# NaN-ignoring row maximum: seven loads, each cut into 27 quarter rows and one quarter row that is itself cut by partitions

## The chip, the cores and the metric

The kernel runs on one core of a Trainium2 chip. A core has engines that each run their own list of instructions and signal each other by semaphores. Four matter here: ScalarE (ACT in the profile), GpSimd (POOL), VectorE (DVE) and SyncE (SP), which here only issues transfers. Sixteen DMA engines move the data between the chip's main memory and the on-chip memory of 128 partitions. The metric is the device time of one execution in microseconds (us). The kernel before has a median of 1252.84 us over three runs (1252.82 to 1252.95).

## The reference

```python
batch, seq, dim = 32, 2048, 2048
x = np.random.randn(batch, seq, dim).astype(np.float32)
mask = np.random.rand(batch, seq, dim) < 0.1
x[mask] = np.nan
...
return np.nanmax(x, axis=axis).astype(np.float32)
```

The axis is the last one. So 65,536 rows of 2,048 floats (537 MB) are read, and one maximum per row is written, NaNs left out.

## The kernel before, in words

**Tiling.** `TILES` is a list of 74 tiles. The unit is a quarter row, `Q` = 512 floats (2,048 bytes). A common tile has 28 quarters, 7 rows, for each of the 128 partitions: 57,344 bytes per partition. A tile is written as three lists, `(loads, pieces, reds)`, whose sums are equal: how the transfer is cut, how the cleaning of NaNs is cut, and how the reductions are cut. The common one is `([28], [7, 9, 12], [16, 12])`: one load, three pieces, two reductions. `GROUPS` joins tiles that share one block of rows; in it each partition owns consecutive rows.

**Stages of a tile.** (1) SyncE issues the tile's loads into one of three buffers `xt` (`BUFS`, line 307). (2) For each piece ScalarE turns the upper 16 bits of each float into a key `kt` (lines 375 and 226), a mapping in which NaN saturates. (3) GpSimd turns the key back into upper bits and writes them into the tile (lines 396 and 236), so that NaNs have become a very low number. A piece with a minus sign in `TILES`, such as the -7 in `[9, 12, -7]`, is turned back by ScalarE itself (`release`, line 350). (4) VectorE reduces the cleaned rows by maximum into `acc` (line 421, noted as line 243). At the end of the rows of some groups `find` marks rows that held only NaNs, and at the very end SyncE stores `acc`.

**What sets the order.** Every engine runs its list in the order of the program text; `Order.add` puts the semaphore waits on. A load waits for two things, `before + lanes[turn]` (line 310): `before` is the last reduction of the tile that used this buffer, three tiles ago; `lanes[turn]` is the transfer that used the same one of 14 landing semaphores (`LANES`), 14 issues ago. A piece on ScalarE waits for the loads that overlap it (`here`, line 365) and for a free key buffer (three of 12 quarters each). A reduction waits for the pieces that it covers.

**Stages of the run.** Tile 0 has one row. Tiles 1 to 47 are common ones, but every eighth (8, 16, 24, 32, 40) is `([28], [9, 12, -7], [8, 20])`, in which ScalarE relieves GpSimd of 7 quarters. Tiles 48 to 61 vary the pieces a little. From tile 62 on the loads are cut smaller and smaller, down to one of 1 quarter (256 KB) in tile 72, and more pieces go back through ScalarE.

The change touches the tiles with the numbers 26, 28, 30, 32, 34, 56 and 58. Before, 26, 28, 30 and 34 are common ones; 32 is `([28], [9, 12, -7], [8, 20])`; 56 is `([28], [7, 9, 12], [12, 16])`; 58 is `([28], [6, 10, 12], [16, 12])`.

Of the kernel before, what the change touches and what calls it, by code (L numbers as in the profile page):

```python
# [8 lines left out]
D = 2048  # L9

Q = D // 4
# [4 lines left out]
TILES = (  # L16
    [([4], [4], [4])]
    + [([28], [7, 9, 12], [16, 12])] * 7
    + [([28], [9, 12, -7], [8, 20])]
    + [([28], [7, 9, 12], [16, 12])] * 7  # L20
    + [([28], [9, 12, -7], [8, 20])]
    + [([28], [7, 9, 12], [16, 12])] * 7
    + [([28], [9, 12, -7], [8, 20])]
    + [([28], [7, 9, 12], [16, 12])] * 7
# [23 lines left out]
)  # L48

GROUPS = [TILES[i : i + 15] for i in range(0, 60, 15)] + [TILES[60:73], TILES[73:]]  # L50


# [12 lines left out]
LANES = 14  # L65
# [7 lines left out]
EDGE = TOP + 0.25  # L73

NONE = -255.0 * 2.0**120


def total(pieces):
    return sum(sum(map(abs, p)) if isinstance(p, tuple) else abs(p) for p in pieces)
# [93 lines left out]
def kernel(  # L173
# [15 lines left out]
    nc = tc.nc  # L189
    P = nc.NUM_PARTITIONS  # L190
# [9 lines left out]
    xr = x.bitcast(i32).flatten_outer_dims()  # L200
    R = xr.shape[0]
    of = out.bitcast(i32).flatten_outer_dims().rearrange("r c -> (r c)")
    rows = [sum(sum(loads) for loads, _, _ in g) * Q // D for g in GROUPS]
    assert R == P * sum(rows)

    sing = ctx.enter_context(tc.tile_pool(name="sing", bufs=1))
# [12 lines left out]
    with tc.tile_critical():  # L219
        order = Order(nc)  # L220
# [61 lines left out]
        number = 0  # L282
        lanes = [[] for _ in range(LANES)]
        turn = 0
# [4 lines left out]
        for gi, (s, g) in enumerate(zip(rows, GROUPS)):  # L289
# [4 lines left out]
            acc = accs[:, first : first + s]  # L294
            base = 0
            for loads, pieces, reds in g:
                assert sum(loads) == total(pieces) == sum(reds)
                xt, before = xts[number % BUFS], free[number % BUFS]
                number += 1
                landed = []  # L300
                at = 0
                for c in loads:
                    c *= Q
                    e = order.add(
                        "sp",
                        nc.sync,
                        lambda: nc.sync.dma_start(  # L307
                            out=xt[:, at : at + c], in_=xg[:, base + at : base + at + c]
                        ),
                        before + lanes[turn],  # L310
                        lane=f"load{turn}",
                        step=16,
                    )
                    lanes[turn] = [e]
                    turn = (turn + 1) % LANES
                    landed.append((at, at + c, e))
                    at += c
                clean = []
                after = []
                at = done = 0  # L320
                reds = [n * Q for n in reds]
                part = []
                held = []
                pairs = {}
                if number not in APART:
                    pairs = joints(pieces, [n // Q for n in reds])
                flat = sum((p if isinstance(p, tuple) else (p,) for p in pieces), ())
                half = {}
                piece = 0

                def cleaned(a, b, k, i, e):

                    nonlocal clock
                    clock += 1
                    both = [(a, b, k, flat[i] < 0, clock)]
                    if i in pairs:
                        if pairs[i] not in half:
                            half[pairs[i]] = both
                            return
                        both += half.pop(pairs[i])  # L340
                    for a, b, k, back, when in both:
                        kfree[k].append((back, when, e))
                        clean.append((a, b, e))

                def name(i):
                    return f"pair{number}_{pairs[i][0]}" if i in pairs else None

                def release():
                    for a, b, k, kp, e, i in held:
                        e = act(  # L350
                            [e],
                            name(i),
                            out=xt[:, a:b].bitcast(i16)[:, 1::2],
                            in_=kp,
                            func=ACT.Copy,
                            bias=float(TOP),
                            scale=-1.0,
                        )
                        cleaned(a, b, k, i, e)
                    held.clear()  # L360

                for parts in pieces:
                    parts = parts if isinstance(parts, tuple) else (parts,)
                    c = int(sum(map(abs, parts))) * Q
                    here = [l for a, b, l in landed if a < at + c and b > at]
                    kold = []
                    if used + c > KEYS:
                        key = (key + 1) % NKEYS
                        used = 0
                        kold, kfree[key] = last(kfree[key]), []  # L370
                        assert all(k != key for q in half.values() for _, _, k, _, _ in q)
                        if at + c == sum(loads) * Q:

                            kold = kold + last(kfree[(key + 1) % NKEYS])
                    e_key = act(
                        here + kold,
                        out=kts[key][:, used : used + c],
                        in_=xt[:, at : at + c].bitcast(i16)[:, 1::2],
                        func=ACT.Prelu,
                        bias=top,  # L380
                        scale=-1.0,
                        alpha=float(TOP - LOW) / (EDGE - NAN),
                    )
                    release()
                    for c in parts:
                        back, wait, c = c < 0, isinstance(c, float), int(abs(c)) * Q
                        kp = kts[key][:, used : used + c]
                        used += c
                        to = xt[:, at : at + c].bitcast(i16)[:, 1::2]
                        at += c  # L390
                        if back:
                            held.append((at - c, at, key, kp, e_key, piece))
                            if not wait or at == sum(loads) * Q:
                                release()
                        else:
                            e = pool(
                                [e_key],
                                name(piece),
                                out=to,
                                in0=kp,  # L400
                                scalar1=-1.0,
                                scalar2=float(TOP),
                                op0=ALU.mult,
                                op1=ALU.add,
                            )
                            cleaned(at - c, at, key, piece, e)
                        piece += 1
                        open_ = [h[0] for h in held] + [p[0] for q in half.values() for p in q]
                        while reds and done + reds[0] <= min([at] + open_):
                            n = reds.pop(0)  # L410


                            lo = done - 1 if done % D else done
                            done += n
                            row = (base + lo) // D
                            if done % D:
                                m, to = 1, xt[:, done - 1 : done].bitcast(f32)
                            else:
                                m = max(n // D, 1)
                                to = acc[:, row : row + m]  # L420
                            e = dve(
                                [e for a, b, e in clean if b > lo and a < done] + part,
                                nc.vector.tensor_reduce,
                                out=to,
                                in_=xt[:, lo:done]
                                .bitcast(f32)
                                .rearrange("p (c d) -> p c d", c=m),
                                axis=mybir.AxisListType.X,
                                op=ALU.max,
                            )  # L430
                            part = [e] if done % D else []
                            after.append(e)
                free[(number - 1) % BUFS] = after[-1:]
                base += at
# [17 lines left out]
        for (og, bits), e in zip(stores, ready):  # L452
# [5 lines left out]
                lane="store",  # L458
# [40 lines left out]
```

## Time and profile before

| | |
|---|---|
| median of three runs | 1252.84 us |
| profiled execution, span from first to last instruction | 1251.3 us |
| VectorE, ScalarE, GpSimd busy | 1110.8, 986.6, 1168.6 us |
| mean duration of a 7, 9 and 12 quarter piece on ScalarE | 3.28, 4.12, 5.41 us |
| the same on GpSimd | 4.20, 5.34, 7.04 us |
| reduction of 16 and of 12 quarters on VectorE | 8.69, 6.54 us |
| read from main memory | 536.87 MB, 429 GB/s over the span |
| loads, and the median from issue to landing of a 28-quarter load | 105; 22.5 us |

The profile comes from one execution with the hardware profiler on; its span has no launch or finish in it, so it is a little shorter than the measured time. Engine names in its lines are ACT, POOL, DVE and SP; SPq is SyncE's queue of transfers. "L236" is the line of the helper that issued the instruction. A line such as `L243 DVE TENSOR_REDUCE acc<-xt` is an operation that reads `xt` and writes `acc`. A load is carried as packets: the trace's records have 128 of them for each load, one per partition, each as long as the partition's part of it. A load has landed when its semaphore has been raised sixteen times, once by each DMA engine; the trace has each of these times.

### The profile page before, as it was taken

To read this page: it belongs to the slowest core of one execution; us is meant where nothing else is said; L and a number is where in the kernel's file an instruction comes from. 1 tells how busy PE (TensorE), PEld (TensorE's weight loads), DVE (VectorE), ACT (ScalarE), POOL (GpSimd) and SP (SyncE) were. 2 spreads that over 40 slices of the span, in tenths; PEclk is the share of its full clock that TensorE was granted. 3 is DMA by queue.
4 is the path that set the end of the run, shared out by engine and by line. 5 is a ranking of instruction groups with operands and counts; after the bars stand their busy time and mean duration, and the time that the engine had idled before them with its cause. 6 is when DMAs were issued, how large, how long until landed. Compare 5 with 4: busy or idle time off the path is not lost.

```text
span 1251.3 us, 893 instructions
## 1 busy us (share of the span) xinstructions
DVE 1110.8 (89%) x181; ACT 986.6 (79%) x273; POOL 1168.6 (93%) x242
## 2 busy tenths in 40 slices
DVE  0888989888889888898988888998888899999999
ACT  3777887778787877788777878777777878999998
POOL 2999989998999899998999899999999999989998
DMA  9999999999999999999999999999999999999997
GB/s 415 440 412 438 440 440 440 411 440 440 440 436 415 440 440 436 438 416 440 440 436 438 416 440 440 436 438 416 440 440 435 440 416 436 436 431 430 428 428 295
DMA packets 15991, 537.20 MB, mean 429 GB/s; under 512 B 2544, under 2 KB 2544, under 8 KB 3568
## 3 DMA queue, kind: packets, MB, share of 16 engines
q1 hardware_dynamic: 15984, 537.14, 99.3%
q14 instruction: 7, 0.06, 0.0%
HBM read 536.87 MB, written 0.26 MB: 429 GB/s over the span
## 4 chain that ended last, share of the span: by engine, by line
DMA 36%; DVE 30%; POOL 20%; ACT 13%; issue 1%; SPq 0%; ACTq 0%
DMA xt<-in_x_dram 36%; DVE acc L243 30%; POOL xt L236 20%; ACT kt L226 11%; ACT xt L226 2%; SPq L307 0%; DVE none L249 0%; DVE acc L263 0%; SPq L494 0%; ACTq L158 0%; SPq L219 0%
## 5 line engine op out<-in xcount | busy, mean ns | idle before, releaser
L236 POOL TENSOR_SCALAR xt<-kt 128x3584 int16<-128x3584 uint16 (+11 forms) x236 | 1167.5, 4947 | 77.9 <-ACT kt L226 60.1
L243 DVE TENSOR_REDUCE acc<-xt 128x3 f32<-128x6144 f32 (+4 forms) x175 | 1107.6, 6379 | 136.7 <-POOL xt L236 128.8
L226 ACT ACTIVATE kt<-xt,scalars 128x3584 uint16<-128x3584 int16 (+9 forms) x247 | 935.3, 3825 | 257.7 <-DMA xt<-in_x_dram 241.6
L226 ACT ACTIVATE xt<-kt 128x512 int16<-128x512 uint16 (+6 forms) x24 | 52.8, 2202 | 0.7
L226 ACT ACT_TABLE_LOAD x1 | 1.3, 1283 | 0.9 <-SPq L219 0.9
L243 DVE TENSOR_REDUCE xt<-xt 128x1 f32<-128x1536 f32 x1 | 1.7, 1745 | 0.0
L269 DVE MEMSET scalars<- 128x1 f32 x1 | 0.1, 59 | 1.0 <-SPq L219 1.0
L249 DVE TENSOR_SCALAR none<-acc 128x414 int32<-128x414 f32 (+1 forms) x2 | 0.8, 380 | 0.1
L263 DVE TENSOR_TENSOR acc<-acc,none 128x414 int32<-128x414 int32 (+1 forms) x2 | 0.7, 374 | 0.1
L249 POOL TENSOR_SCALAR late<-acc 128x91 int32<-128x91 f32 x1 | 0.5, 545 | 0.1
L263 POOL TENSOR_TENSOR acc<-acc,late 128x91 int32<-128x91 int32 x1 | 0.3, 340 | 0.1
L480 POOL MEMSET const-float32-0.0<- 128x1 f32 x1 | 0.1, 98 | 0.2 <-issue 0.2
L226 ACT ACTIVATE scalars<-scalars 128x1 f32<-128x1 f32 x1 | 0.2, 203 | 0.0
L480 POOL MEMSET const-bfloat16-1.0<- 128x1 bf16 x1 | 0.1, 101 | 0.0
L480 POOL MEMSET const-uint8-127<- 128x1 uint8 x1 | 0.1, 101 | 0.0
L480 POOL MEMSET const-float32-1.0<- 128x1 f32 x1 | 0.1, 99 | 0.0
## 6 DMA issues: line engine op xcount, KB each, us to landing
xt<-in_x_dram SPq DMA_DIRECT2D x61, 7168.0 KB, 22.5
xt<-in_x_dram SPq DMA_DIRECT2D x2, 5120.0 KB, 17.3
xt<-in_x_dram SPq DMA_DIRECT2D x3, 2816.0 KB, 22.5
xt<-in_x_dram SPq DMA_DIRECT2D x4, 2048.0 KB, 22.2
xt<-in_x_dram SPq DMA_DIRECT2D x5, 1536.0 KB, 29.0
xt<-in_x_dram SPq DMA_DIRECT2D x2, 3584.0 KB, 24.6
xt<-in_x_dram SPq DMA_DIRECT2D x6, 1024.0 KB, 26.6
xt<-in_x_dram SPq DMA_DIRECT2D x3, 1792.0 KB, 29.9
```

The source lines that it names most:

```text
L226: lambda: nc.scalar.activation(**kw),
L236: lambda: nc.gpsimd.tensor_scalar(**kw),
L243: return order.add("dve", nc.vector, lambda: do(**kw), deps)
L249: lambda: engine.tensor_scalar(out=none, in0=acc, scalar1=NONE, scalar2=float(0x00800000), op0=ALU.is_equal, op1=ALU.mult,),
L263: lambda: engine.tensor_tensor(out=bits, in0=bits, in1=none, op=op),
L269: e_top = order.add("dve", nc.vector, lambda: nc.vector.memset(top, EDGE), [])
L480: nc = _bacc.Bacc("TRN2", target_bir_lowering=False, num_devices=1)
```

## The change

Seven tiles get a common new form: loads of 27 quarters and of 1 quarter, pieces of 7, 9 and 12, reductions of 16 and 12. A load may now be a pair `(quarters, runs)`; the runs are numbers of partitions that add up to 128, and each run becomes a transfer of its own. So the last quarter row of the seven tiles comes in two transfers, the first for partitions 0 to 119, 125, 116, 107 or 87, the second for the rest. All other lines of the diff follow from the new form of `loads`: a helper `width` adds the quarters up.

```diff
+def parted(*runs):
+    return [([27, (1, runs)], [7, 9, 12], [16, 12])]
+
+
+for number, runs in (
+    (26, (120, 8)),
+    (28, (126, 2)),
+    (30, (117, 11)),
+    (32, (108, 20)),
+    (34, (88, 40)),
+    (56, (120, 8)),
+    (58, (126, 2)),
+):
+    TILES = TILES[:number] + parted(*runs) + TILES[number + 1 :]
...
+def width(loads):
+    return sum(c[0] if isinstance(c, tuple) else c for c in loads)
...
                 for c in loads:
+                    c, runs = c if isinstance(c, tuple) else (c, (P,))
+                    assert sum(runs) == P
                     c *= Q
-                    e = order.add(
-                        "sp",
-                        nc.sync,
-                        lambda: nc.sync.dma_start(
-                            out=xt[:, at : at + c], in_=xg[:, base + at : base + at + c]
-                        ),
-                        before + lanes[turn],
-                        lane=f"load{turn}",
-                        step=16,
-                    )
-                    lanes[turn] = [e]
-                    turn = (turn + 1) % LANES
-                    landed.append((at, at + c, e))
+                    p = 0
+                    for n in runs:
+                        e = order.add(
+                            "sp",
+                            nc.sync,
+                            lambda: nc.sync.dma_start(
+                                out=xt[p : p + n, at : at + c],
+                                in_=xg[p : p + n, base + at : base + at + c],
+                            ),
+                            before + lanes[turn],
+                            lane=f"load{turn}",
+                            step=16,
+                        )
+                        lanes[turn] = [e]
+                        turn = (turn + 1) % LANES
+                        landed.append((at, at + c, e))
+                        p += n
                     at += c
```

In the order of instructions, SyncE has 14 more transfers, ScalarE one operation fewer (the -7 of tile 32) and GpSimd one more; VectorE has as many as before.

More of the change, by code (lines that the diff above doesn't have):

```diff
@@ L202 @@
     of = out.bitcast(i32).flatten_outer_dims().rearrange("r c -> (r c)")
-    rows = [sum(sum(loads) for loads, _, _ in g) * Q // D for g in GROUPS]
+    rows = [sum(width(loads) for loads, _, _ in g) * Q // D for g in GROUPS]
     assert R == P * sum(rows)
@@ L296 @@
             for loads, pieces, reds in g:
-                assert sum(loads) == total(pieces) == sum(reds)
+                assert width(loads) == total(pieces) == sum(reds)
                 xt, before = xts[number % BUFS], free[number % BUFS]
@@ L371 @@
                         assert all(k != key for q in half.values() for _, _, k, _, _ in q)
-                        if at + c == sum(loads) * Q:
+                        if at + c == width(loads) * Q:
                             kold = kold + last(kfree[(key + 1) % NKEYS])
@@ L392 @@
                             held.append((at - c, at, key, kp, e_key, piece))
-                            if not wait or at == sum(loads) * Q:
+                            if not wait or at == width(loads) * Q:
                                 release()
```

## The prediction

> **What bounds the kernel now.** I read the page first (span, busy shares, DMA queues), then busy time by stretch, the waits, the chain that ended last, and GpSimd's timeline around tile 32.
>
> ```profile
> span 1251.3 us, 893 instructions
> ...
> DVE 1110.8 (89%) x181; ACT 986.6 (79%) x273; POOL 1168.6 (93%) x242
> ...
> q1 hardware_dynamic: 15984, 537.14, 99.3%
> q14 instruction: 7, 0.06, 0.0%
> ```
>
> No compute engine is full, but the load queue is: its packets take 99.3% of 16 DMA engines' span, first fill and tail included. By stretch (the last two columns are the DMA share and GB/s):
>
> ```profile
> 442.00:459.00 17.00, 15.15 (x2) 12.88 (x4) 16.72 (x4) 1.00 1.00 432
> 600.00:769.20 169.20, 151.57 (x21) 131.41 (x32) 161.59 (x30) 1.00 1.00 434
> 1100.00:1235.00 135.00, 134.95 (x40) 129.35 (x60) 125.91 (x42) 1.00 1.00 429
> ```
>
> The middle stretch is ten tiles of 28 quarter rows, 16.92 us each. DMA share is 1.00 throughout; the small loads near the end cost 1% of rate (429). The waits and SyncE's own waits:
>
> ```profile
> ACT kt L226 <- DMA xt<-in_x_dram: 241.6, 62, 14.9
> ...
> SPq L307 <- DVE acc L243: 1156.1, 71, 37.8
> ```
>
> ScalarE waits for nearly every landing: compute follows the data. SyncE waits for DVE to free a buffer, which looks like a loop through compute, and the chain (start, us, what) shows the same alternation:
>
> ```profile
> 508.17 22.50 DMA xt<-in_x_dram
> ...
> 530.70 3.29 ACT kt L226
> ...
> 534.06 4.20 POOL xt L236
> ...
> 538.34 5.34 POOL xt L236
> ...
> 543.71 15.16 DVE acc L243 x2
> ...
> 558.88 22.50 DMA xt<-in_x_dram
> ```
>
> But its 22.50 us from issue to landing holds only 16.92 us of transfer; 5.6 us are spent behind the load before. That 5.6 us is the cover: a load may be issued so much later before the queue runs dry. So the DMA engines set the end, and what counts is the busiest one. The trace's packet records give 2,116 ns for 57,344 bytes, 84 ns for 2,048; each load's semaphore gets 16 part-landings, one per engine. Of the last load's, twelve fall within 0.22 us and four at 0.70, 0.99, 1.16 and 1.25 us after the first: some engines lag. The lag appears after the q14 packets at 246 and 255 us (two part-landings 0.6 us behind in the next load) and grows after those at 386, 940, 999 and 1130 us. The mean of the sixteen is 0.33 us, so perfect evening-out would gain 1.25 - 0.33 = 0.92 us, no more.
>
> **The change, part by part.** Span 1251.3, outside it 1252.84 - 1251.3 = 1.5 us, kept.
>
> *Loads.* Seven loads of 28 quarter rows become 27 + 1, the 1 in two. Bytes are unchanged. SyncE issues 14 more DMAs; the trace's issues run 0.33 us, so 4.6 us in all, two per tile behind a first issue which keeps the queue fed: hidden by the 5.6 us cover (uncovered, 0.66 us per tile). Lanes rotate over 14 semaphores and 14 issues are added, so every later load keeps its lane, and the transfer 14 issues back has long landed. ScalarE's first two pieces (0 to 16 quarters) need only the 27-quarter load, which lands one quarter sooner; the third piece waits for all three, and starts 3.29 + 4.12 = 7.4 us after the first landing: hidden.
>
> *Which engine carries what.* No load of this trace has fewer than 128 partitions. The first parts are 15x8, 14x9, 13x9, 12x9 and 11x8; I assume n partitions go evenly to the largest number of engines up to 16 that divides n, always starting with the same engine. Then the seven first parts put 8, 9, 9, 9, 8, 8, 9 packets on it and the second parts (8, 2, 11, 20, 40, 8, 2) add 1, 1, 1, 2, 4, 1, 1: 71 packets instead of 56, while the last engine gets none. The nearest row for such a packet is the 128x512 load near the end: 0.63 us from the landing before it to its own, 79 ns per packet. The same bytes inside a long packet take 2,116 / 28 = 75.6 ns. So the busiest engine gains 71 x 79 - 56 x 75.6 = 1.4 us. If it is one of the twelve prompt ones, the end moves by 0.2 + 1.4 - 1.25, about 0.3; if one of the four laggards, 1.4. I take 1.0. The floor is the 0.92 gain above.
>
> The Trainium skill, DMA: Bandwidth & Descriptors, section on why a DMA increments its semaphore by 16, states that deal (largest k up to 16 that divides, lowest-numbered engines); the sixteen part-landings of each load agree for 128 partitions, and no run here shows another count.
>
> *Engines meeting on one path.* Today all sixteen engines end their equal packets together, at 27.1 GB/s each, with a fixed set of 8 partitions each. With 8 or 9 partitions dealt another way, two engines may write into one set while another set gets nothing. No row shows it. Lower bound 0: the 128x512 load pays nothing. Upper bound: a quarter row takes three times its 0.63 us, 7 x 1.26 = 8.8 us. A lag once made is never recovered, since each engine is busy to the end. By size, the nearest row is the free one, but it has the orderly deal that the change gives up; so I go some way up, 0.4 us per split, 2.8 us.
>
> The Trainium skill, SBUF — State Buffer, section on the DMA port swizzle, has partitions p and p+32 behind one port of about 27 GB/s and 64 partitions loading at little over half the rate of 128. The trace's 27.1 GB/s per engine agrees with one engine per port; no run here shows two. By it, blocks of 8 neighbouring partitions put two engines on each port, a quarter takes twice as long, and the estimate is 7 x 0.63 = 4.4 us, in place of 2.8.
>
> *Side effects of the common entry.* Tile 32 loses its back piece: 7 quarters move from ScalarE (4.20 us) to GpSimd (4.20 us).
>
> ```profile
> 534.06 16.77 POOL L236 TENSOR_SCALAR xt<-kt 128x3584 int16<-128x3584 uint16 x3 [0.16 <-ACT kt L226]
> 551.82 12.47 POOL L236 TENSOR_SCALAR xt<-kt 128x4608 int16<-128x4608 uint16 x2 [0.98 <-ACT kt L226]
> 567.91 21.06 POOL L236 TENSOR_SCALAR xt<-kt 128x3584 int16<-128x3584 uint16 x4 [3.62 <-ACT kt L226]
> ```
>
> GpSimd idles 0.98 and 3.62 us around it; a common tile would run 550.9 to 567.7, just before 567.9. Hidden; if not, the cover takes it (4.2 < 5.6). Tile 56's reductions swap (8.7 us first, then 6.5): DVE ends about 0.6 us sooner, no one waits. Tile 58's first piece grows from 6 to 7 quarters with the same total. All nothing.
>
> Sum: 1251.3 + 1.0 + 2.8 = 1255.1, plus 1.5: **1256.6 us**.
>
> **Rivals.**
>
> *No meeting, packets only.* If a path takes two engines in turn without loss, only the 0.3 to 1.4 us are left: 1253.1 to 1254.3. For it: 27.1 GB/s looks like each engine's own pace, as the q14 packets of 8,192 bytes run at the same (309 ns). Against it: nothing seen tells engine from path. Not slower by a measurable amount: it wins wherever meeting costs less than about 0.2 us per split.
>
> *Evening-out works.* The relieved engines are the four laggards, and the added packets run hidden beside others: the end comes up to 0.92 us sooner, 1251.9 to 1252.8. Against it: the last engine would be relieved by 56 x 75.6 ns = 4.2 us where the worst lag is 1.25, so most of the relief is unusable, and the load goes onto the engines that then end last.
>
> *Few engines carry a part.* If only powers of two are dealt, 120, 126, 117, 108 and 88 partitions go to 8, 2, 1, 4 and 8 engines: 15 + 63 + 117 + 27 + 11 + 15 + 63 = 311 packets on the first, and 25 of the second parts: 336 x 79 ns - 4.2 = 22 us more, 1275. Against it: the odd splits would have no sense.
>
> **Numbers.** The forecast (meeting costs something) 0.52, its own range 1255.0 to 1262.5; packets only 0.38; evening-out 0.06; few engines 0.04. A measurement of this kernel can tell about 0.2%, 2.5 us. Slower by more: 0.51 of the forecast's 0.52 and 0.04 of few engines, 0.55. Faster by more would need beyond the floor that I worked out: 0.03. Within: 0.42. The range runs from inside the evening-out case, 1252.6, to 1251.3 + 1.5 + 0.9 + 8.8, 1262.5; outside it lie few engines and bits of the two others.
>
> **What would show it.** In the changed kernel, the part-landings of the load after each split tell which engines are late and by how much: a spread that grows by about 0.5 us at each of the seven tiles is meeting; one that grows by 0.1 to 0.3 us is packets only; a single part-landing 5 us behind is few engines. Long 2,048-byte packets (well over 84 ns) speak for meeting. GpSimd's idle time before tile 33 should go to nearly nothing, and SyncE should still wait for DVE. I am wrong if the spread shrinks, or if the time moves while the DMA share falls below 1.00 in the middle, which would mean that a buffer wait, not an engine, set it.

## The result and the profile after

The changed kernel has a median of 1260.65 us over four runs (1260.14 to 1260.78), the kernel before 1252.89 us beside it. The ratio is 1.006, with a 95% interval of 1.0049 to 1.0072: slower by 7.8 us, clear of the noise and well inside the range, but twice the 3.8 us that the forecast added. Two executions of the experiments below, one of 1291.15 and one of 1347.95 us, are far slower than the others of their kernels and are left out of the medians. The profiled execution has a span of 1259.0 us, 7.7 us more than before. The page of the changed kernel:

```profile
span 1259.0 us, 914 instructions
...
DVE 1110.8 (88%) x181; ACT 982.6 (78%) x272; POOL 1172.8 (93%) x243
...
q1 hardware_dynamic: 17025, 537.14, 99.4%
```

VectorE has the same work, GpSimd 4.2 us more and ScalarE 4.0 us less (tile 32's piece). The load queue is as full as before. What the page doesn't say at first sight is that the full queue moved less. Busy time by stretch of the changed kernel, over tiles 26 to 36 and over a stretch without split tiles (the last two columns are the DMA share and GB/s):

```profile
425.00:629.00 204.00, 177.16 (x24) 152.00 (x38) 190.88 (x36) 1.00 1.00 424
640.00:800.00 160.00, 144.23 (x20) 126.15 (x31) 152.69 (x29) 1.00 1.00 434
```

and the same two stretches of the kernel before:

```profile
425.00:629.00 204.00, 181.19 (x25) 161.06 (x39) 192.43 (x36) 1.00 1.00 435
640.00:800.00 160.00, 142.38 (x20) 123.70 (x29) 152.63 (x28) 1.00 1.00 433
```

The share is 1.00 in all four, and the rate falls from 435 to 424 only where the split tiles are. A DMA engine that is slowed counts as busy; the rate, not the share, shows it. The missing 11 GB/s are worth 204 us x 11 / 435 = 5.2 us in this stretch. The landings say the same more exactly: beside the kernel before, the whole of tile 25 lands 0.12 us later; 27, 29, 31, 33 and 35, each the tile after a split one, land 1.07, 2.19, 3.31, 4.55 and 5.91 us later. Then nothing changes for twenty tiles (5.80 us at tile 55), tiles 57 and 59 stand at 6.62 and 7.68, and the last load of all at 7.69. So each split costs 0.8 to 1.4 us, for good, and the tail only shifts. The engines lose it nearly together: the mean of tile 35's sixteen part-landings comes 5.04 us later than before where the last one comes 5.91 us later. Dealing the same bytes unevenly would move the last part-landing but hardly the mean, so it can have added no more than about 0.9 us by then.

The waits of ScalarE and of SyncE in the changed kernel, and the chain of waits around tiles 31 to 34 (start, us, what):

```profile
ACT kt L246 <- DMA xt<-in_x_dram: 252.9, 63, 14.9
```

```profile
SPq L331 <- DVE acc L263: 1156.0, 71, 37.8
```

```profile
509.52 24.46 DMA xt<-in_x_dram
...
534.00 3.29 ACT kt L246
...
537.37 4.19 POOL xt L256
...
541.64 5.34 POOL xt L256
...
547.01 15.16 DVE acc L263 x2
...
562.18 24.11 DMA xt<-in_x_dram
```

ScalarE waits 11.3 us longer for landings (252.9 against 241.6). SyncE waits for VectorE as long as before (1156.0 against 1156.1), and the compute links of the chain are unchanged; its DMA links grew from 22.50 to 24.46 and 24.11 us. The loss is in the transfers.

**Which engine carries what** can be read from the part-landings. A load on 128 partitions raises its semaphore 16 times as data land. The split loads raise it fewer times, after one early raise within 0.2 us of the end of the issue:

```
partitions   120  8  126  2  117  11  108  20  88  40
late raises   15  8   14  2   13  11   12  10  11  10
```

This is the deal that the prediction assumed, and that the Trainium skill states (DMA: Bandwidth & Descriptors, section on why a DMA increments its semaphore by 16): the largest number up to 16 that divides the partitions, the rest of the raises written at once by the issuer. The trace agrees in all ten loads of the first five split tiles.

**Where the time sits** is in the packet records. In the kernel before every 2,048-byte packet took 84 ns and 42 of 7,808 full packets (57,344 bytes, 2,116 ns) ran long, by which I mean 10 ns or more, up to 2,647 ns. In the changed kernel the 896 short packets average 113 ns, up to 196, and 207 of 6,912 full ones run long, up to 3,208 ns. From 455 to 490 us, one split tile and its neighbours, the excess per engine (summed over all packets and divided by sixteen, since the records don't say which engine carried a packet) is 0.27 us in short packets, 0.05 us in those of 55,296 bytes and 0.67 us in full ones, which belong to whole loads next to the split one. So around this split two thirds of the price is paid by transfers that the change didn't touch. Over the whole run the excess is 1.6, 0.4 and 5.2 us beyond that of the kernel before, 7.2 of the 7.8 us.

### The profile page after: what moved, and what is told of

Same layout as the page of the kernel before. It is cut to its first block, busy times and chain, and to the rows that moved or that the text cites. A ratio compares the mean times of both kernels' runs of the same rounds, so it can differ in the third digit from the quotient of the medians.

```text
span 1259.0 us, 914 instructions
## 1 busy us (share of the span) xinstructions
DVE 1110.8 (88%) x181; ACT 982.6 (78%) x272; POOL 1172.8 (93%) x243
## 4 chain that ended last, share of the span: by engine, by line
DMA 36%; DVE 32%; POOL 20%; ACT 11%; issue 1%; SPq 0%; ACTq 0%
DMA xt<-in_x_dram 36%; DVE acc L263 32%; POOL xt L256 20%; ACT kt L246 10%; ACT xt L246 1%; SPq L331 0%; DVE none L269 0%; DVE acc L283 0%; SPq L520 0%; ACTq L178 0%; SPq L239 0%
## 5 line engine op out<-in xcount | busy, mean ns | idle before, releaser
L256 POOL TENSOR_SCALAR xt<-kt 128x4608 int16<-128x4608 uint16 (+9 forms) x237 | 1171.7, 4944 | 81.4 <-ACT kt L246 63.7
L263 DVE TENSOR_REDUCE acc<-xt 128x4 f32<-128x8192 f32 (+4 forms) x175 | 1107.5, 6380 | 144.5 <-POOL xt L256 138.2
L246 ACT ACTIVATE kt<-xt,scalars 128x3584 uint16<-128x3584 int16 (+9 forms) x247 | 935.4, 3826 | 269.3 <-DMA xt<-in_x_dram 252.9
L246 ACT ACTIVATE xt<-kt 128x512 int16<-128x512 uint16 (+6 forms) x23 | 48.6, 2114 | 0.7
```

The costliest lines, as they stand in the source:

```text
L246: lambda: nc.scalar.activation(**kw),
L256: lambda: nc.gpsimd.tensor_scalar(**kw),
L263: return order.add("dve", nc.vector, lambda: do(**kw), deps)
```

## The experiments

Three theories. *Meeting*: an engine that writes into partitions which another engine serves in a full load slows that one and itself. *Small loads*: short packets, or more transfers, cost the time. *Uneven deal*: the busiest engine's extra packets cost it. The medians are each beside the kernel before on the same chip. Of each experiment's edit against the changed kernel only the lines that matter are shown.

**Side effects alone.**

```diff
-    return [([27, (1, runs)], [7, 9, 12], [16, 12])]
+    return [([28], [7, 9, 12], [16, 12])]
```

> The seven tiles get the common pieces and reductions but keep one load of 28 quarters: the side effects alone. Every theory of the transfers: as before, 1252.6 to 1253.3 us. If the lost back piece of tile 32 or the other reductions cost the time: towards 1260.7.

Measured: 1253.04 us against 1253.08; ratio 1.000 (0.9991 to 1.0009). The lost back piece of tile 32 and the other reductions cost nothing.

**As many loads, all on 128 partitions.**

```diff
-    return [([27, (1, runs)], [7, 9, 12], [16, 12])]
+    return [([26, 1, 1], [7, 9, 12], [16, 12])]
```

> Loads of 26, 1 and 1 quarters, each on all 128 partitions: as many transfers as in the changed kernel and more short packets, but the usual deal. Meeting on a path: only packets and semaphores, about 0.15 to 0.2 us per tile, 1253.8 to 1254.4 us. Small transfers or their number cost the time: about 1260.7 us.

Measured: 1254.28 us against 1253.08; 1.001 (1.0001 to 1.0020). All 1,792 short packets of these tiles take 84 ns. Fourteen more loads cost 1.2 us, not 7.8: small loads are not the cause.

**Two halves of 64 partitions.**

```diff
-    return [([27, (1, runs)], [7, 9, 12], [16, 12])]
+    return [([27, (1, (64, 64))], [7, 9, 12], [16, 12])]
```

> The quarter row in two loads of 64 partitions: every engine gets 4 + 4 packets, so no engine carries more, but not the partitions it usually has. Meeting: about 1.0 us per tile, 1258.5 to 1262 us. Uneven deal (the busiest engine's extra packets cost the time): 1253 to 1254.3 us.

Measured: 1259.85 us against 1253.08; 1.0056 (1.0040 to 1.0073). The same two stretches of this run and then of the run with 26 + 1 + 1:

```profile
425.00:629.00 204.00, 177.98 (x24) 152.86 (x38) 191.72 (x36) 1.00 1.00 423
640.00:800.00 160.00, 144.23 (x20) 126.17 (x31) 152.75 (x29) 1.00 1.00 432
```

```profile
425.00:629.00 204.00, 180.74 (x25) 156.78 (x38) 196.27 (x37) 1.00 1.00 432
640.00:800.00 160.00, 142.37 (x20) 123.97 (x29) 152.76 (x28) 1.00 1.00 432
```

Each engine has the same bytes in the same number of loads in both runs, and here it has only half as many short packets (896 against 1,792 in all). What is new is which engine has which partition, and the rate falls to 423 in the split stretch alone. The short packets average 120 ns, and at each of the first five splits 16 full packets run long, as many as there are engines. The whole tiles after the five splits land 1.12, 2.10, 3.05, 4.02 and 5.00 us later than before while the sixteen part-landings there stay within 1.2 us: all engines lose alike. So an uneven deal isn't needed for this loss. If the splits of the changed kernel meet as much as the halves do, 7.8 - 6.8 = 1.0 us is left for it; no run has it alone.

**Four times the bytes through the same splits.**

```diff
-    return [([27, (1, runs)], [7, 9, 12], [16, 12])]
+    return [([24, (4, runs)], [7, 9, 12], [16, 12])]
```

> The same splits, but with 24 + 4 quarters, so four times the bytes go through split loads in as many transfers. Meeting: the loss goes with the bytes, 4 x 7.7 = 31 us, about 1284 us (1275 to 1290). A price per transfer: 1260 to 1262 us. Uneven deal alone: 15 x 4 x 75.6 ns = 4.5 us and some, 1257 to 1259 us.

Measured: 1284.44 us against 1253.08; 1.0254 (1.0239 to 1.0270), 31.4 us more: four times 7.8 is 31.2. The price goes with the bytes, not with the number of loads. The first stretch of this run:

```profile
425.00:629.00 204.00, 165.25 (x22) 139.04 (x35) 174.01 (x33) 1.00 1.00 392
```

**Does the address of the partition matter?** The next runs change which partitions stand together in a load. In each the quarter row comes in nine loads, or eight. Where a load is given as (first partition, number, step), the loop takes partitions at that step; that edit of the loop is not shown.

```diff
# step of 4
+    return [([27, (1, tuple((i, 8, 4) for i in (0, 1, 2, 3, 32, 33, 34, 35)) + ((64, 64, 1),))], [7, 9, 12], [16, 12])]
# neighbours
+    return [([27, (1, tuple((i, 8, 1) for i in range(0, 64, 8)) + ((64, 64, 1),))], [7, 9, 12], [16, 12])]
# mirror image
+    return [([27, (1, tuple((64 + i, 8, 4) for i in (0, 1, 2, 3, 32, 33, 34, 35)) + ((0, 64, 1),))], [7, 9, 12], [16, 12])]
```

> The quarter row in nine loads: partitions 0 to 63 in eight loads of 8 partitions at a step of 4 (i, i+4, ... i+28), partitions 64 to 127 in one. If the address of a partition sets its path as the Trainium skill's page on SBUF has it (p and p+32 on one path, four neighbours on one path), the eight loads put each of eight engines on the path that it uses anyway; what is left is meeting in the last load and an uneven deal (12 packets instead of 8 on eight engines): 1256 to 1260 us. If it is not the partition but the number of partitions below 128 that costs: the same as the two runs beside it.

> As the run beside it, with the same number of loads, packets and engines, but the eight loads take 8 neighbouring partitions each, so four engines stand on one path. Meeting by partition: 3 to 6 us more than with the step of 4, 1260 to 1266 us. Number of partitions or loads: the same within 1 us.

> The mirror image of the run with the step of 4: partitions 64 to 127 in eight loads of 8 at a step of 4, partitions 0 to 63 in one load. Same loads, same packets per engine, but by the page's map all of the eight loads go to paths that eight other engines use. Meeting by partition: 3 to 6 us more than its mirror image, 1260 to 1266 us. Number of partitions or loads: the same within 1 us.

Measured against 1253.15 us: 1265.55 (1.0097, 1.0081 to 1.0113), 1265.87 (1.0101, 1.0086 to 1.0116) and 1269.66 us (1.0140, 1.0124 to 1.0156). The step of 4 missed its 1256 to 1260 us by far, and the neighbours weren't 3 to 6 us behind it. The mirror image was, by 4.1 us, with the same loads and the same packets for each engine. So the partitions matter, but these runs have too much else in them: an uneven deal, and a last load of 64 partitions that meets. The run without that last load, and so without that half of the quarter row, has less in it (the 0.044 us per load that it expects comes from the run of eight full loads further down):

```diff
+    return [([27, (1, tuple((i, 8, 4) for i in (0, 1, 2, 3, 32, 33, 34, 35)))], [7, 9, 12], [16, 12])]
```

> Leaves out the quarter row of partitions 64 to 127 in the seven tiles; partitions 0 to 63 get theirs in eight loads of 8 partitions at a step of 4. By the page's map no engine then writes on another one's path, though no short load has more than 8 partitions and eight engines have nothing in them. Meeting by partition: every 2,048-byte packet keeps its 84 ns and the long ones 2,116 ns; the eight engines carry as many bytes as before in 63 more loads... by the 0.044 us per load of the eight full quarter loads 56 more loads cost 2.5 us: 1253 to 1256 us. If it is loads on few partitions or on few engines that cost: packets grow as in the mirror images (mean well over 84 ns), and 1257 us or more in spite of the missing bytes.

Measured: 1254.99 us against 1253.13; 1.0015 (1.0005 to 1.0024). Of 448 short packets 445 keep 84 ns, though every short load uses eight partitions. The eight loads of the step of 4 therefore meet next to nobody, and a load on few partitions isn't slow by itself. That the last load then costs over 10 us more, where two such loads alone cost 6.8, is only partly explained: in the run with the step of 4 some engines have run ahead, so that the first part-landing of tile 26's last load comes 2.9 us before the last one of its eight short loads, and 285 full packets run long against 156 with the two halves. Full packets also ran long here (146, up to 4,265 ns), for which I have no reason; engines ran ahead here too, with a spread of the part-landings of 3.5 us at tile 35, as in the first point of the last section.

**The same with an even deal.** Eight loads of 16 partitions give each of sixteen engines one packet per load:

```diff
# neighbours
+    return [([27, (1, (16,) * 8)], [7, 9, 12], [16, 12])]
# the price of a load, all partitions
+    return [([20] + [1] * 8, [7, 9, 12], [16, 12])]
# step of 4
+    return [([27, (1, tuple((i, 16, 4) for i in (0, 1, 2, 3, 64, 65, 66, 67)))], [7, 9, 12], [16, 12])]
```

> The quarter row in eight loads of 16 neighbouring partitions: one packet on each of 16 engines, so the deal is even, but four engines on one path at a time. Meeting: at least the loss of the two halves, 1259 to 1264 us. Uneven deal: 1253.5 to 1255 us.

> Loads of 20 quarters and eight times 1 quarter, all on 128 partitions: nine loads per tile in the usual deal, as many as in the runs with eight short loads. The price of a load by itself: the run with 26 + 1 + 1 paid 1.2 us for 14 more loads, 0.086 us each; 56 more make 4.8 us, about 1257.9 us. If a load costs nothing by itself and all of the loss of the short loads is meeting: 1253.5 to 1255 us.

> The quarter row in eight loads of 16 partitions at a step of 4 (i to i+60, then i+64 to i+124): one packet on each of 16 engines, as with 16 neighbours, but by the page's map half of the packets stay on the path that their engine uses anyway, instead of 8 of 128. Meeting by partition: between the run of eight full quarter loads and the 1261.4 us of the 16 neighbours, about 1259 to 1260 us. If the partitions' addresses don't matter: 1261.4 us, within 0.5.

> The eight loads of 16 neighbours once more, beside the two runs above on one chip: 1261 to 1262 us by every theory; it is here so that the difference to the step of 4 is taken on the same chip.

Measured: neighbours 1261.43 us against 1253.15 (1.0067, 1.0051 to 1.0084), then, on one chip against 1253.16: eight full loads 1255.64 (1.0019, 1.0011 to 1.0028), step of 4 1259.37 (1.0051, 1.0037 to 1.0064), neighbours again 1261.98 (1.0085, 1.0070 to 1.0099; the median lies at the low end of this, since the executions scatter upwards). The first stretch of these three:

```profile
425.00:629.00 204.00, 180.22 (x24) 155.40 (x38) 194.88 (x36) 1.00 1.01 431
```

```profile
425.00:629.00 204.00, 179.16 (x24) 154.00 (x38) 192.88 (x36) 1.00 1.00 426
```

```profile
425.00:629.00 204.00, 177.15 (x24) 151.97 (x38) 190.84 (x36) 1.00 1.01 423
```

The full loads cost 2.5 us for 56 more loads, 0.044 us each, half of what I expected, and none of 7,168 short packets ran long. Neighbours and step of 4 have equal loads, packets and engines, and differ by 2.6 us on one chip by their medians, by about 4 us by their ratios, and by 2.1 us from the first run of the neighbours. The size is uncertain, since the repeat of the neighbours scattered from 1261.5 to 1266.7 us, but of the executions in these medians none of the neighbours is below 1261.1 us and none of the step of 4 above 1260.0. The short packets average 119 and 96 ns. Which partitions an engine gets changes the price at an equal deal.

Take the Trainium skill's map (SBUF — State Buffer, section on the DMA port swizzle) and assume that neighbouring partitions are dealt in blocks, which no run shows. The estimate is then that 120 of the 128 packets of the 16 neighbours go on a path that another engine serves, 64 with the step of 4, 64 in the two halves, 110 to 117 in the five splits and none in the run without its last load. The order of the losses beyond the price of the loads agrees for the neighbours, the step of 4 and the run without its last load; the map doesn't give their sizes: the two halves lose nearly as much as the splits with half as many packets astray. In the three runs with a last load of 64 partitions the estimate is 32, 88 and 96, and the first two lost the same, 12.4 and 12.7 us, which the map leaves open. The path itself is in no record; that it lies at the destination is the Trainium skill's statement, and I didn't try to separate it from the source rows, which change with the partitions. So it is shown that the deal of partitions to engines costs the time, and argued that the cost arises where two engines write to one place.

## Why the prediction was right, and which term was too small

*What bounds the kernel.* Right: compute hid every shift, SyncE's wait for VectorE stayed at 1156 us, and what the last landing had lost was kept but for 0.1 us.

*Which engine carries what.* Right in the number of engines, by the raises. That it is always the same engines is in no record, but the spread that grows from split to split speaks for it. The term, 1.0 us with 1.4 at most, fits: full loads of the same number cost 1.2, the splits cost 1.0 more than the even halves, and after five splits the last part-landing had lost 0.9 us more than the mean. It wasn't measured alone.

*Meeting.* Right in kind, too small in size, and this is the term that made the sum 4 us short. I took 0.4 us per split, 2.8 in all. The two halves, less the price of their loads, give 6.8 - 1.2 = 5.6 us, 0.8 per split; in the changed kernel 7.8 less the packets' 1.0 to 1.4 leaves 6.4 to 6.8, over 0.9 per split. I had priced only the quarter row's own slowing, between nothing and 1.26 us per split, and stayed low because the nearest row by size, the 128x512 load, paid nothing. The short packets did not even double (113 ns for 84). The larger part falls on the full packets that they meet, 0.67 of 0.99 us per engine around one split, and that I left out. The Trainium skill's rule on ports, by which I had put 4.4 us beside my 2.8, was the better guide and still too low for the same reason. That the range held is in part luck: its upper end let the quarter row take three times its time, and the loss came mostly from packets that it didn't count. (That end, 1262.5, also adds 0.9 us for the packets where the sum has 1.0; nothing hangs on it.)

*Rivals.* Packets only: the run with 26 + 1 + 1 comes nearest to it, though with an even deal: 1254.3 us, at the upper end of its 1253.1 to 1254.3, and 6.4 us short of the changed kernel. Few engines: excluded by the raises. Evening-out: it failed in its premise too. In tile 26 of the changed kernel each of the three loads has one part-landing alone at its end, 0.8 to 1.0 us behind the next, and the latest of all is in the load of 8 partitions, 0.19 us after the last one of the 120. So the engine that lagged most was, as it seems, among the eight that were given more, not the one that was spared.

*Side effects.* Nothing, as costed (1253.04 us). I had expected GpSimd's idle time before tile 33 to go to nearly nothing. GpSimd around tiles 31 to 33 of the changed kernel, and from tile 32 on in the run with the side effects alone:

```profile
537.37 16.77 POOL L256 TENSOR_SCALAR xt<-kt 128x3584 int16<-128x3584 uint16 x3 [0.99 <-ACT kt L246]
554.57 16.77 POOL L256 TENSOR_SCALAR xt<-kt 128x3584 int16<-128x3584 uint16 x3 [0.43 <-ACT kt L246]
572.43 16.76 POOL L256 TENSOR_SCALAR xt<-kt 128x3584 int16<-128x3584 uint16 x3 [1.09 <-ACT kt L246]
```

```profile
550.91 50.59 POOL L256 TENSOR_SCALAR xt<-kt 128x3584 int16<-128x3584 uint16 x9 [0.15 <-ACT kt L246]
```

With the side effects alone it went from 3.62 us to nothing, nine operations in a row, as expected. In the changed kernel it went to 1.09 us, since the data of tile 33 came late as well. That was a by-product of the loss which I hadn't carried through.

*Signs named in advance.* "A spread that grows by about 0.5 us at each split" came true at the first five splits, by 0.3 to 0.8 us each: the spread of the sixteen part-landings of whole loads went 1.26, 1.57, 2.25, 3.01, 3.83, 4.25 us. But the spread is a poor sign for meeting: in the two halves it stayed at 1.2 us while the loss was nearly as large, and in the changed kernel it shrank again after the fifth split while the loss stayed. The last landing is the one to read. Long 2,048-byte packets did show it. The DMA share stayed at 1.00 and SyncE still waited for VectorE, as named.

No run beat the kernel before. Since the whole gain to be had was 0.92 us, and a split costs more (about 1 us) than it takes off the spared engine (0.6 us), I tried none that aims at single engines.

## What to carry to other kernels

When a queue of full-width loads is the bound, a load on part of the partitions isn't priced by its own bytes: 256 KB through another deal cost about 1 us here, more than the 0.6 us that the same bytes take in all, and most of it was paid by neighbouring full loads. Read the rate beside the DMA share, since a slowed engine counts as busy, and follow the last landing tile by tile to see which load lost what. To relieve one engine, first find out which engine lags: here the relief went to others.

## What the runs showed that I had not expected

- Engines that run ahead are slowed without any short load near. In the changed kernel the spread of the part-landings falls from 4.25 us at tile 35 to about 2.4 us at tile 47, and full packets of up to 3,208 ns stand between 680 and 720 us, while the last landing keeps its distance to the kernel before (5.91 to 5.80 us). What holds the leaders back stays open.
- A load's own price, on 128 partitions, was 0.086 us for 14 more loads and 0.044 us for 56 more.
- A load of one packet per engine took 0.2 us from one last landing to the next (447.07, 447.26, 447.45, 447.64 us with the step of 4 in tile 26), where the packet takes 84 to 159 ns. It isn't all lost: in the run without its last load the steps are 0.19 us too, and tile 26 lands 0.95 us later than before, but the whole tile 27 only 0.16 us.
